# The down projection of a SwiGLU feed-forward layer as seven block products instead of eight, with its operands streamed from DRAM

## The chip, the cores and the metric

The kernel runs on one core of one Trainium2 chip. The time is device microseconds of one execution of the whole kernel, from a launch to its end. Before the change it took 2273.01 us, the median of three runs (2272.06 to 2274.47).

## The reference

The reference is one inference step of a two-layer decoder trunk over 1024 prompt tokens and 64 sample tokens (1088 rows), D_MODEL = 1024, all in float32. Layer 0 is a gMLP mixer, layer 1 a sliding-window attention; each has a SwiGLU feed-forward (D_FF = 2816) behind it, in sandwich RMSNorm:

```
def swiglu_ffn(h, w_gate, w_up, w_down):
    return (jax.nn.silu(h @ w_gate) * (h @ w_up)) @ w_down
...
        h = rms_norm(x, f_norm_pre[layer])
        x = x + rms_norm(swiglu_ffn(h, f_w_gate[layer], f_w_up[layer], f_w_down[layer]), f_norm_post[layer])
```

The change is about the last product, hidden (1088 x 2816) times `f_w_down` (2816 x 1024), which is done twice, once in each layer.

## The kernel before

**Number format.** Every large product is done in three matmuls. A float32 operand is split into a high part (ScalarE, L275 or L510, a copy into the rounded format) and a low part (VectorE, L276 or L511, the difference), and high*high, low*high and high*low are summed in one PSUM bank. A matmul here has a 128x128 stationary and a 128x512 moving operand.

**Gate and up.** `ffn` (L1080) walks 22 steps q: gate and up weights of a pair of feature tiles in turn. Each step already uses a seven-product scheme (`part` called from `p1`, `p2`, `p657`, `p4`, `p3`). The hidden values of a pair of feature tiles (two tiles of 128 features, 1024 prompt tokens) stand in two `rows` tiles, of which there are two, so that the next pair's first write (the `keep` copy at L1117) waits until this pair's stores have landed. `store` (L1092) writes each 128x512 block to a DRAM tensor `hid`, one for each feature tile, four blocks for a pair.

**Down.** Below the gate and up steps, `fetch` (L1211) loads whole feature tiles of the hidden rows back (L1218) and splits them; `W` (class `Weights`) loads, splits and hands out the tiles of `f_w_down`, up to six ahead (`W.cap`). The 22 feature tiles go in six groups (`GROUPS`). For each group, each of the eight token blocks (and the sample rows as a ninth) and each half of the output columns, `down` (L1223) sums the group's products in one bank, and the bank is added to an accumulator in SBUF (L1240; L1238 copies in the first group). So the prompt takes 22 x 8 x 2 x 3 = 1056 matmuls in a layer and the sample rows 22 x 2 x 2 = 88, all at L1235.

**What follows.** In the last group, each finished block goes through `Exit.second` (L1037): sum of squares on ScalarE (L1040), the root on GpSimd (L863), two passes on VectorE (L1042, L1043), and a store. In layer 0 a second norm follows (squares, root, scaled copy), and once three blocks are there `Exit.turn` (L1057) turns them with transposes on TensorE and splits them for the key, value and query products, which take the token ranges c = 0, 1, 2 in this order. In layer 1 the store of the last block ends the kernel.

**What sets the order.** `Flow` keeps a clock of TensorE work as the program is written, and `flow.later(ns, fn)` puts side work that many nanoseconds on. The tile framework then places each engine's instructions by its own timeline. All DMAs are issued from SyncE, in order, and a DMA that waits holds up those behind it. The big SBUF tiles come from one pool of 40 (`act_tile`); PSUM has five banks called `bank` and three called `aux`.

## Time and profile before

| what | value |
|---|---|
| profiled execution | 2275.59 us, span 2273.9 us |
| median of three runs | 2273.01 us |
| TensorE (PE) busy | 2202.6 us, 97% of the span, 11392 matmuls |
| weight loads (PEld) | 1864.3 us, 82%, beside the matmuls |
| VectorE (DVE) busy | 1283.2 us, 56% |
| ScalarE (ACT) busy | 810.4 us, 36% |
| DMA | 194.69 MB, mean 86 GB/s |
| down projection, layer 0 / layer 1 | 855.9 to 1126.7 us / 1999.8 to 2264.2 us |

The profile is one execution, taken by the hardware profiler. Instructions stand under the line of the kernel that issued them. Matmuls overlap: one takes 0.39 us from end to end, but a new one starts every 0.23 us, so busy time and not the mean is what a matmul costs. "Idle before, releaser" names what an engine waited for ahead of a group. The granted clock of TensorE is given as a share of full speed. A "chain of waits" follows the last instruction back through whatever released each step.

### The profile page before, as it was taken

The page shows a single profiled execution, that of the slowest core. Times are in us where ns is not written, and L with a number is a line of the kernel's source. Part 1 is how long each engine was busy: PE and PEld are TensorE (multiplying, and loading weights), DVE is VectorE, ACT ScalarE, POOL GpSimd, SP SyncE. Part 2 cuts the span into 40 slices and gives each one's busy share as a digit, 9 for nine tenths or more (in the row PEclk, how much of TensorE's full clock was granted, in tenths as well). Part 3 has the DMA queues.
Part 4 walks back from the last instruction along what each step waited for, and adds up shares of the span by engine and source line. Part 5 has one row for each costly group of instructions (what it writes and reads, how often), then busy time and mean ns, then how long its engine had stood idle before and what let it go on. Part 6 is the DMA issues. An engine that isn't in the chain of part 4 may idle for free.

```text
span 2273.9 us, 29115 instructions
## 1 busy us (share of the span) xinstructions
PE 2202.6 (97%) x11392; PEld 1864.3 (82%) x11392; DVE 1283.2 (56%) x2081; ACT 810.4 (36%) x1647; POOL 182.3 (8%) x222
## 2 busy tenths in 40 slices
PE   8999996999999999999999999969999999999998
PEld 7999875888888887888898877758888888878886
DVE  5465448655655653545757774477565565535446
ACT  5234424322322333211566762234232332342112
POOL 2322210000000000000213320110000000000000
PEclk9999998999999999999999998979999999999999
DMA  4211332122222234223441111221222221343224
GB/s 147 57 38 38 96 106 86 61 71 90 76 64 89 76 106 138 91 77 104 136 118 43 47 60 57 98 88 64 74 85 63 80 86 62 97 143 109 77 86 143
DMA packets 138975, 194.69 MB, mean 86 GB/s; under 512 B 22051, under 2 KB 101653, under 8 KB 138838
## 3 DMA queue, kind: packets, MB, share of 16 engines
q1 hardware_dynamic: 138838, 192.84, 26.8%
q8 instruction: 89, 1.46, 0.3%
q14 instruction: 48, 0.39, 0.1%
HBM read 143.88 MB, written 43.32 MB: 82 GB/s over the span
## 4 chain that ended last, share of the span: by engine, by line
PE 73%; DVE 5%; DMA 3%; ACT 2%; issue 1%; SPq 0%; POOL 0%; POOLq 0%; ACTq 0%; DVEq 0%
PE bank L1235 22%; PE bank L1076 11%; PE bank L1077 11%; PE bank L1078 11%; PE bank L1138 2%; PE bank L1137 2%; PE bank L873 2%; PE bank L874 1%; PE bank L505 1%; PE bank L504 1%; PE bank L506 1%; PE bank L875 1%; DVE act L276 1%; DMA act<-hid 1%; DMA raw<-in_f_w_down 1%
## 5 line engine op out<-in xcount | busy, mean ns | idle before, releaser
L1235 PE MATMUL bank<-act,act 128*128 128x512 f32 x2288 | 526.5, 392 | 5.9 <-ACT act L510 5.3
L1076 PE MATMUL bank<-act,act 128*128 128x512 f32 x1232 | 487.0, 396 | 31.0 <-ACT rows L1117 17.9
L276 DVE TENSOR_TENSOR act<-raw,act 128x1024 fp32r<-128x1024 f32 x261 | 317.5, 1223 | 352.0 <-PE bank L1077 188.3
L1235 PEld LDWEIGHTS bank<-act,act 128*128 128x128 f32 x2288 | 430.0, 189 | 100.7 <-ACT act L510 7.8
L275 ACT ACTIVATE act<-raw 128x1024 fp32r<-128x1024 f32 x261 | 275.2, 1059 | 597.7 <-PE bank L1235 203.9
L1077 PE MATMUL bank<-act,act 128*128 128x512 f32 x1232 | 485.2, 394 | 0.0
L1078 PE MATMUL bank<-act,act 128*128 128x512 f32 x1232 | 478.6, 391 | 1.2 <-DVE act L276 1.2
L1076 PEld LDWEIGHTS bank<-act,act 128*128 128x128 f32 x1232 | 232.8, 189 | 78.4 <-ACT rows L1117 18.3
L1078 PEld LDWEIGHTS bank<-act,act 128*128 128x128 f32 x1232 | 232.6, 189 | 51.0 <-DVE act L276 2.7
L1077 PEld LDWEIGHTS bank<-act,act 128*128 128x128 f32 x1232 | 233.2, 189 | 43.1
L1240 DVE TENSOR_TENSOR act<-bank,act 128x512 f32<-128x512 f32 x180 | 123.5, 688 | 150.9 <-PE bank L1235 150.7
L504 PE MATMUL bank<-act,act 128*128 128x384 f32 (+1 forms) x624 | 205.8, 332 | 2.0 <-DVE act L636 1.4
L506 PE MATMUL bank<-act,act 128*128 128x384 f32 (+1 forms) x624 | 206.8, 332 | 0.4 <-DVE act L276 0.4
L505 PE MATMUL bank<-act,act 128*128 128x384 f32 (+1 forms) x624 | 206.4, 331 | 0.0
L863 POOL TENSOR_TENSOR tok<-tok,expo 128x1 f32<-128x1 f32 (+1 forms) x63 | 54.5, 866 | 1719.3 <-DVE tok L862 1719.3
L504 PEld LDWEIGHTS bank<-act,act 128*128 128x128 f32 x624 | 117.7, 189 | 4.0 <-DVE act L636 1.6
L506 PEld LDWEIGHTS bank<-act,act 128*128 128x128 f32 x624 | 117.6, 189 | 1.9 <-issue 1.2
L505 PEld LDWEIGHTS bank<-act,act 128*128 128x128 f32 x624 | 117.8, 189 | 1.0 <-issue 0.7
L873 PE MATMUL bank<-act,act 128*128 128x512 f32 (+1 forms) x288 | 114.9, 402 | 0.6 <-DVE tok L899 0.6
L874 PE MATMUL bank<-act,act 128*128 128x512 f32 (+1 forms) x288 | 113.7, 395 | 0.0
L875 PE MATMUL bank<-act,act 128*128 128x512 f32 (+1 forms) x288 | 111.8, 393 | 0.0
L511 DVE TENSOR_TENSOR act<-act,act 128x64 fp32r<-128x64 f32 (+3 forms) x114 | 71.9, 657 | 49.9 <-ACT act L510 49.3
(231 smaller groups left out, 2628.0 us busy)
## 6 DMA issues: line engine op xcount, KB each, us to landing
act<-hid SPq DMA_DIRECT2D x44, 544.0 KB
raw<-in_f_w_gate SPq DMA_DIRECT2D x44, 512.0 KB
raw<-in_f_w_up SPq DMA_DIRECT2D x44, 512.0 KB
hid<-rows SPq DMA_DIRECT2D x88, 256.0 KB
raw<-in_f_w_down SPq DMA_DIRECT2D x44, 512.0 KB
stream<-act SPq DMA_DIRECT2D x24, 512.0 KB
rows<-stream SPq DMA_DIRECT2D x24, 512.0 KB
raw<-in_sg_w_in SPq DMA_DIRECT2D x16, 512.0 KB
```

Of the source, the lines that this page charges most:

```text
L275: nc.scalar.activation(self.hi, raw, AF.Copy)
L276: nc.vector.tensor_tensor(self.lo, raw, self.hi.bitcast(F32), op=ALU.subtract)
L504: nc.tensor.matmul(out[:, :n], h, xh[:, cs:cs + n], start=begin, stop=False)
L505: nc.tensor.matmul(out[:, :n], h, xl[:, cs:cs + n], start=False, stop=False)
L506: nc.tensor.matmul(out[:, :n], l, xh[:, cs:cs + n], start=False, stop=end)
L873: nc.tensor.matmul(ps[:m, :], xh, h, start=begins and j == 0, stop=False)
L874: nc.tensor.matmul(ps[:m, :], xl, h, start=False, stop=False)
L875: nc.tensor.matmul(ps[:m, :], xh, l, start=False, stop=ends and j == len(todo) - 1)
L1076: nc.tensor.matmul(ps, h, xh, start=begin and k == 0, stop=False, skip_group_check=not begin)
L1077: nc.tensor.matmul(ps, h, xl, start=False, stop=False, skip_group_check=not begin)
L1078: nc.tensor.matmul(ps, l, xh, start=False, stop=k == 3, skip_group_check=not begin)
L1235: nc.tensor.matmul(ps, x, w, start=i == j == 0, stop=i == n - 1 and j == len(todo) - 1)
```

## The change

With the feature tiles of a pair called 1 and 2, the first and second 512 tokens x and y, and the first and second 512 output columns u and v, the down projection becomes a 2 x 2 block product. It is now done in seven products by Strassen's scheme (in Winograd's form), each over 11 pairs and four token blocks: x1 u1, x2 u2, s3 t3, s2 t2, y2 t4, s1 t1, s4 v2, with s1 = y1+y2, s2 = s1-x1, s3 = x1-y1, s4 = x2-s2, and t1 = v1-u1, t3 = v2-v1, t2 = t3+u1, t4 = u2-t2.

- **Sums of the hidden blocks.** `sums` makes s1 to s4 of a pair after its last block (four 128x512 operations on VectorE); seven blocks of a pair are stored (x1, x2, y2, s1, s2, s3, s4) in place of four. The `rows` tiles of a pair are now taken at `p2`, and the `keep` copy of `p1` goes to a temporary.
- **Streaming.** Each product runs through six units of two pairs (the last of one). `send` loads a unit's hidden blocks and one or two quarter blocks of `f_w_down`; `make` splits the hidden blocks, forms t1 to t4 on VectorE, and splits the weights. Up to four units are sent ahead and two made ahead. `f_w_down` no longer goes through `W`, whose `cap` is 0 until the last product.
- **Sums in PSUM.** Four banks hold the four token blocks of a product through all 11 pairs; x2 u2 adds to the banks of x1 u1, and s1 t1 and s4 v2 add to those of s2 t2. `gather` joins products on ScalarE or VectorE, 28 times in a layer; the additions at L1240 are gone. The sample rows go with x1 u1, x2 u2, s1 t1 and s4 v2.
- **Exit.** `Exit` is split in `first` (the first half of the columns, after y2 t4) and `second`. Blocks 4 to 7 finish after s1 t1, blocks 0 to 3 after s4 v2, whose last four units are run block by block. In layer 0 the order of the last blocks is 3, 0, 1, 2, and the key, value and query products take the token ranges in the order 2, 1, 0.

The matmuls of a prompt layer come to 7 x 11 x 4 x 3 = 924 in place of 1056, those of the sample rows stay 88. The diff, cut to its core:

```
@@ -29,9 +29,11 @@
-GROUPS = [3, 3, 4, 4, 4, 4]
+SENT = 4
+STREAMED = 4
 ORDER = [0, 1, 2, 3, 8, 4, 5, 6, 7]
+CORDER = [2, 1, 0]
...
     def add_ffn(layer):
         for q in range(NF):
             W.add_quad(a[("f_w_gate", "f_w_up")[q % 2]][layer], q // 2 * 2, (layer, q))
-        for f in range(NF):
-            W.add(a["f_w_down"][layer][f * P:(f + 1) * P, :], 1, D)
...
+        def first(self, b, z):
+            m = tokens(b)
+            j = tmp()[:m, :]
+            nc.scalar.activation(j, z[:m, :HN], AF.Square, accum_out=tok[:m, 0, b:b + 1])
+            nc.vector.tensor_tensor(z[:m, :HN], z[:m, :HN], self.post[:m, :HN], op=ALU.mult)
+            nc.vector.tensor_scalar(tok[:m, 1, b:b + 1], tok[:m, 0, b:b + 1], 1.0 / D, EPS, op0=ALU.mult, op1=ALU.add)
...
         def second(self, b, z):
             m = tokens(b)
             h = act_tile()[:, :D]
             z, r = z[:m, :], self.r.pop(b)[:m, :]
-            nc.scalar.activation(h[:m, :], z, AF.Square, accum_out=tok[:m, 2, b:b + 1])
-            rs = inverse(b, 3, tok[:m, 2, b:b + 1], EPS)
-            nc.vector.scalar_tensor_tensor(z, z, rs, self.post[:m, :], op0=ALU.mult, op1=ALU.mult)
-            nc.vector.tensor_tensor(z, z, r, op=ALU.add)
+            nc.scalar.activation(h[:m, :HN], z[:, HN:], AF.Square, accum_out=tok[:m, 2, b:b + 1])
+            nc.vector.tensor_tensor(z[:, HN:], z[:, HN:], self.post[:m, HN:], op=ALU.mult)
+            rs = inverse(b, 3, tok[:m, 2, b:b + 1], tok[:m, 1, b:b + 1])
+            nc.vector.scalar_tensor_tensor(z, z, rs, r, op0=ALU.mult, op1=ALU.add)
...
-            if c == 0:
+            if k == len(self.x):
                 self.x.append(act_pair())
...
-        hid = [mk(dpool, [P, T], F32, f"hid{layer}_{f}") for f in range(NF)]
+        hid = {n: mk(dpool, [P, NF // 2, HN], F32, f"hid{layer}_{n}") for n in ("x1", "x2", "y2", "s1", "s2", "s3", "s4")}
+        hsm = mk(dpool, [P, 2, NF // 2, NS], F32, f"hid{layer}_smp")
...
         def store(q, i, c):
-            nc.sync.dma_start(hid[q // 2 * 2 + i][:, c * HN:(c + 1) * HN], region(q, i, c))
+            if i or not c:
+                nc.sync.dma_start(hid[("x" if c == 0 else "y") + str(i + 1)][:, q // 2, :], region(q, i, c))
+        def sums(q):
+            p = q // 2
+            x1, y1, x2, y2 = (region(q, i, c) for i in range(2) for c in range(2))
+            t = act_tile()
+            s1, s2 = t[:, :HN], t[:, HN:D]
+            for n, o, u, v, op in (("s1", s1, y1, y2, ALU.add), ("s3", y1, x1, y1, ALU.subtract),
+                                   ("s2", s2, s1, x1, ALU.subtract), ("s4", x1, x2, s2, ALU.subtract)):
+                nc.vector.tensor_tensor(o, u, v, op=op)
+                nc.sync.dma_start(hid[n][:, p, :], o)
...
         def p1(q):
             need("x1")
-            if q % 2 == 0:
-                rows[q // 2] = [special([P, D], "rows", bufs=2) for _ in range(2)]
+            if q == 0:
+                rows[0] = new_rows()
             s = st[q]
             s["a"] = bank()
             part(s["a"], unit(q, "b1"), 0, ent, "x1", True)
-            s["keep"] = region(q, 0, 1) if q % 2 == 0 else tmp()
+            s["keep"] = region(q, 0, 1) if q == 0 else tmp()
             nc.scalar.activation(s["keep"], s["a"], AF.Copy)
 
         def p2(q):
             need("x2")
             s = st[q]
             part(s["a"], unit(q, "b2"), 0, ent, "x2", False)
+            if q % 2 == 0 and q:
+                rows[q // 2] = new_rows()
             r = region(q, 0, 0)
             if q % 2 == 0:
                 nc.scalar.activation(r, s["a"], AF.Silu)
...
-                for i in range(2):
-                    nc.sync.dma_start(hid[q // 2 * 2 + i][:, SEQ:], r[:, i, :])
+                nc.sync.dma_start(hsm[:, :, q // 2, :], r)
...
             take(q, 0, 1, s["c"], s["u2"])
+            if q % 2:
+                sums(q)
...
+        wd = a["f_w_down"][layer].rearrange("(q i p) n -> p q i n", i=2, p=P)
+        order = [("x1", "u1"), ("x2", "u2"), ("s3", "t3"), ("s2", "t2"), ("y2", "t4"), ("s1", "t1"), ("s4", "v2")]
+        NP = NF // 2
+        units = [(hn, wn, e, min(2, NP - e)) for hn, wn in order for e in range(0, NP, 2)]
+        loaded, ready, chained, smps, ext = deque(), deque(), {}, {}, []
+        sent, made = [0], [0]
+        def send():
+            hn, wn, e, n = units[sent[0]]
+            sent[0] += 1
+            lo = act_tile(F32R)[:, :n * HN]
+            load(lo.bitcast(F32), hid[hn][:, e:e + n, :], n)
+            raws = []
+            for name in {"t3": ("v2", "v1"), "t2": ("u1",), "t4": ("u2",), "t1": ("v1", "u1")}.get(wn, (wn,)):
+                raws.append(act_tile()[:, :n * HN])
+                load(raws[-1], quarter(name, e, n), n)
+            loaded.append((lo, raws))
...
+        def make():
+            hn, wn, e, n = units[made[0]]
+            made[0] += 1
+            lo, raws = loaded.popleft()
+            hi = act_tile(F32R)[:, :n * HN]
+            split(hi, lo, lo.bitcast(F32))
+            c = raws[0]
+            if wn in ("t3", "t1"):
+                nc.vector.tensor_tensor(c, c, raws[1], op=ALU.subtract)
+            elif wn == "t2":
+                c = chained[e]
+                nc.vector.tensor_tensor(c, c, raws[0], op=ALU.add)
+            elif wn == "t4":
+                nc.vector.tensor_tensor(c, c, chained.pop(e), op=ALU.subtract)
+            if wn == "t3":
+                chained[e] = c
+            wh, wl = (t[:, :n * HN] for t in act_pair())
+            split(wh, wl, c)
+            ready.append((hi, lo, wh, wl))
...
+        def supply():
+            while sent[0] < min(len(units), made[0] + SENT):
+                send()
+            make()
...
+        def sample_rows(i):
+            smps[i] = []
...
+                nc.sync.dma_start(raw, hsm[:, i, e:e + n, :])
+                split(sm[:, :, 0, :], sm[:, :, 1, :], raw)
+                smps[i].append(sm.rearrange("p f s t -> p f (s t)"))
...
+            for e in range(n):
+                xh, xl = (t[:, e * HN + i * P:e * HN + (i + 1) * P] for t in (hi, lo))
+                h, l = (t[:, e * HN:(e + 1) * HN] for t in (wh, wl))
+                for k, (x, w) in enumerate([(xh, h), (xl, h), (xh, l)]):
+                    nc.tensor.matmul(ps, x, w, start=begin and e == k == 0, stop=end and e == n - 1 and k == 2,
+                                     skip_group_check=adds)
...
+            def gather(hn, i, ps):
+                (x0, x1), (y0, y1) = half[i], half[4 + i]
+                if hn in ("x1", "x2"):
+                    nc.scalar.activation(x1 if hn == "x1" else x0, ps, AF.Copy)
+                else:
+                    d, t = {"s3": (y1, x1), "s2": (y0, y1), "y2": (y0, y0), "s1": (y1, y1), "s4": (x1, x1)}[hn]
+                    nc.vector.tensor_tensor(d, ps, t, op=ALU.add)
...
+            rest = ([0, 1, 2, 3] if last else [3, 0, 1, 2])
...
+            for j, (hn, wn, e, n) in enumerate(units):
+                begin, end = e == 0, e + n == NP
+                if begin:
+                    if hn in ("x1", "s2"):
+                        A = [bank() for _ in range(4)]
+                    if hn in ("s3", "y2"):
+                        B = [bank()] + [aux() for _ in range(3)]
+                    if hn in ("x1", "s1"):
+                        sb = aux()
+                    if hn in ("x1", "x2"):
+                        sample_rows(int(hn[1]) - 1)
...
+                    if hn == "s4":
+                        W.cap = 2
+                        W.prepare()
+                u = ready.popleft()
+                if made[0] < len(units):
+                    supply()
...
+                if hn == "s4" and e >= STREAMED:
+                    kept.append((u, n, end))
+                    if not end:
+                        continue
+                    for i in rest:
+                        for u, n, end in kept:
+                            product(ps[i], i, u, n, False, end, True)
+                        gather(hn, i, ps[i])
+                        finish(i, acc[i])
+                        flow.run()
+                    continue
+                for i in range(4):
+                    product(ps[i], i, u, n, begin and not adds, end, adds)
+                    if end:
+                        gather(hn, i, ps[i])
+                        if hn == "y2":
+                            ext[0].first(4 + i, acc[4 + i])
+                            ext[0].first(i, acc[i])
+                        if hn == "s1":
+                            finish(4 + i, acc[4 + i])
+                    flow.run()
+            W.cap = 4
+            W.prepare()
...
+            if (fn, q) == (p2, NF - 1):
+                W.cap = 0
+                down_begin()
...
+        down()
+        return ext[0]
...
-    for c in range(3):
+    for c in CORDER:
...
-            if c == 2:
+            if c == CORDER[-1]:
```

Two places of the order are spoken of below. The first is SyncE at the start of the down projection of layer 0. `hid0_20` and `hid0_21` are the last two feature tiles, `rs` the sample rows' hidden values; the rows of before are:

```order
L1218 DMA act_1078_7005<-hid0_0_527_3407 128x1088
L349 DMA raw_1066_6992<-in_f_w_down 128x1024
L1093 DMA hid0_21_548_3428<-rows_1012_6630 128x512
L1218 DMA act_1080_7012<-hid0_1_528_3408 128x1088
L1093 DMA hid0_21_548_3428<-rows_1012_6630 128x512
L1163 DMA hid0_20_547_3427<-rs_1035_6802 128x64
L1163 DMA hid0_21_548_3428<-rs_1035_6802 128x64
L1093 DMA hid0_20_547_3427<-rows_1011_6629 128x512
L1218 DMA act_1082_7019<-hid0_2_529_3409 128x1088
```

The sample rows' part went to the same tensors as the rest, two DMAs for a pair. Now, at the same place, `hid0_smp` is a tensor of its own, stored for all pairs and read back at once (L1289):

```order
L1106 DMA hid0_x1_527_3407<-rows_1026_6771 128x512
L1243 DMA act_1059_6949<-hid0_x1_527_3407 128x1024
L1243 DMA act_1060_6951<-in_f_w_down 128x2x512
L1106 DMA hid0_y2_529_3409<-rows_1027_6772 128x512
L1106 DMA hid0_x2_528_3408<-rows_1027_6772 128x512
L1191 DMA hid0_smp_534_3414<-rs_1041_6868 256x1x64
L1289 DMA tmp_1090_7087<-hid0_smp_534_3414 128x512
L1289 DMA tmp_1092_7092<-hid0_smp_534_3414 128x192
L1289 DMA tmp_1124_7322<-hid0_smp_534_3414 128x512
L1289 DMA tmp_1126_7327<-hid0_smp_534_3414 128x192
L1117 DMA hid0_s1_530_3410<-act_1074_7063 128x512
L1243 DMA act_1093_7096<-hid0_x1_527_3407 128x512
```

The stores of the last pair are mixed with the loads of the first product, whose operand x1 was stored long before, and four reads of the sample rows follow their last store directly.

The second place is TensorE at the end of the down projection of layer 0. L1235 is the down projection of before, L1062 are transposes of `turn`, L504 and L505 the key products. Before:

```order
L1235 MATMUL bank_8760<-act_8370,act_8140 128x512
L1062 MATMUL aux_8664<-ident_70,act_8425 128x128
L1062 MATMUL aux_8664<-ident_70,act_8466 128x128
L1062 MATMUL aux_8664<-ident_70,act_8507 128x128
L1235 MATMUL bank_8833<-act_8078,act_8119 128x512
L1235 MATMUL bank_8833<-act_8078,act_8120 128x512
...
L1235 MATMUL bank_8847<-act_8369,act_8141 128x512
L1235 MATMUL bank_8847<-act_8370,act_8140 128x512
L504 MATMUL bank_8899<-act_8593,act_8375 128x384
L505 MATMUL bank_8899<-act_8594,act_8375 128x384
L506 MATMUL bank_8899<-act_8593,act_8376 128x384
```

The transposes stood among the matmuls of the down projection, and the last of these was followed by key products. After, where L1303 is the down projection and L1070 the transposes:

```order
L1303 MATMUL bank_7787<-act_8631,act_8543 128x512
L1303 MATMUL bank_7787<-act_8632,act_8628 128x512
L1070 MATMUL aux_8775<-ident_70,act_8670 128x128
L1070 MATMUL aux_8775<-ident_70,act_8474 128x128
L1070 MATMUL aux_8775<-ident_70,act_8491 128x128
...
L1070 MATMUL aux_8807<-ident_70,act_8525 128x128
L1070 MATMUL aux_8807<-ident_70,act_8694 128x64
L1070 MATMUL aux_8813<-ident_70,act_8670 128x128
L1070 MATMUL aux_8813<-ident_70,act_8474 128x128
L1070 MATMUL aux_8813<-ident_70,act_8491 128x128
L504 MATMUL bank_8940<-act_8779,act_6903 128x320
L504 MATMUL bank_8975<-act_8779,act_8536 128x320
```

Eighteen transposes now stand between the last matmul of the down projection and the first key product, and the rest of the turning goes on among the key products.

More of the change, by code (lines that the diff above doesn't have):

```diff
@@ L1104, in take, with new_rows @@
                 store(q, i, c)
+        def new_rows():
+            return [special([P, D], "rows", bufs=2) for _ in range(2)]
         def need(name):
@@ new lines, in down_begin, with product @@
+        def down_begin():
+            for i in range(2):
+                supply()
+        def product(ps, i, u, n, begin, end, adds):
+            hi, lo, wh, wl = u
+            for e in range(n):
[4 more added lines that the diff above has]
+                                     skip_group_check=adds)
+            flow.pe(n * 3 * HN / 2.4)
@@ L1242, in folded @@
-        def folded():
-            for h in range(2):
-                ps = bank()
-                nc.tensor.matmul(ps[:NS, :], fold, acc[NB][:, h * HN:(h + 1) * HN], start=True, stop=True)
-                nc.scalar.activation(z8[:NS, h * HN:(h + 1) * HN], ps[:NS, :], AF.Copy)
-            flow.pe(1800)
-            ext.second(NB, z8)
-        fetch(0)
-        for gi, gn in enumerate(GROUPS):
-            xs, hs = parts.popleft()
-            us = [W.get() for _ in range(gn)]
-            order = list(range(NB + 1))
-            final = gi == len(GROUPS) - 1
-            if final:
-                W.cap = 5
-                ext = Exit(lambda b: ent.out[:tokens(b), b, :], ("f_norm_post", layer), last)
-                order = [NB] + order[:-1] if last else order[:6] + [NB] + order[6:-1]
-                ext.fetch(order[0])
-                z8 = act_tile()[:, :D]
-            for j, b in enumerate(order):
-                if final and j < NB:
-                    ext.fetch(order[j + 1])
-                for h in range(2):
-                    down(b, h, us, xs, hs, gi)
-                    if j == NB and h:
-                        for u in us:
-                            W.done(u)
-                    flow.run()
-                if j == 0 and not final:
-                    fetch(gi + 1)
-                if final and b < NB:
-                    ext.second(b, acc[b])
-                elif final:
-                    flow.later(K["zsum"], folded)
@@ L1277, in ffn @@
-        return ext
+        down()
+        return ext[0]
     def widen():
```

89 lines of the change are left out of this document (57 added, 32 removed).

## The prediction

> **What bounds the kernel now.** I read the page first: the busy times, the chain that ended last, and the largest group.
>
> ```profile
> PE 2202.6 (97%) x11392; PEld 1864.3 (82%) x11392; DVE 1283.2 (56%) x2081; ACT 810.4 (36%) x1647; POOL 182.3 (8%) x222
> PE 73%; DVE 5%; DMA 3%; ACT 2%; issue 1%; SPq 0%; POOL 0%; POOLq 0%; ACTq 0%; DVEq 0%
> L1235 PE MATMUL bank<-act,act 128*128 128x512 f32 x2288 | 526.5, 392 | 5.9 <-ACT act L510 5.3
> ```
>
> TensorE is busy for 97% of the span and carries the chain. The group that the change rewrites, L1235, holds 526.5 us, and TensorE idled only 5.9 us ahead of it. Then the windows by stage (gate and up, down, and what follows, in layer 0; gate and up, down in layer 1) say whether other engines have room there.
>
> ```profile
> core 0: us, PE busy (x) PEld busy (x) DVE busy (x) ACT busy (x) POOL busy (x), PEclk, DMA share, GB/s
> 410.00:856.00 446.00, 443.43 (x2127) 371.85 (x2125) 258.57 (x348) 140.50 (x205) 0.00 (x0) 1.00 0.26 81
> 856.00:1127.00 271.00, 268.02 (x1173) 219.42 (x1174) 132.50 (x187) 75.28 (x116) 7.78 (x11) 0.99 0.31 106
> 877.00:1127.00 250.00, 250.00 (x1111) 205.81 (x1110) 122.86 (x172) 66.41 (x99) 7.78 (x11) 1.00 0.28 96
> 1127.00:1200.00 73.00, 73.00 (x463) 70.56 (x462) 45.98 (x90) 50.72 (x114) 14.98 (x16) 1.00 0.45 121
> 1552.00:1995.00 443.00, 441.65 (x2121) 370.63 (x2120) 257.20 (x345) 139.98 (x204) 0.00 (x0) 1.00 0.25 78
> 2025.00:2264.00 239.00, 239.00 (x1051) 196.54 (x1050) 118.58 (x161) 50.62 (x74) 4.40 (x8) 1.00 0.30 101
> ```
>
> Behind its first 20 us the down projection runs with TensorE busy for 250.00 of 250.00 us and 239.00 of 239.00, at full granted clock. VectorE has half of that time free, ScalarE more, the DMA engines some 70%. So a matmul less is time less, as long as the new work of the others stays under the rate of the matmuls.
>
> **Matmuls.** A layer loses 1056 - 924 = 132, both 264. One costs 526.5/2288 = 0.230 us of busy time; the window 2025:2264 gives 239.00/1051 = 0.227. That is -59.9 to -60.7; I take **-60.0**. All of it lies on the path.
>
> **Start of the down projection.** The timeline of TensorE there, start and length in us, and two windows:
>
> ```profile
> 855.93 7.71 PE L1235 MATMUL bank<-act,act 128*128 128x512 f32 x30 [1.18 <-ACT act L510]
> 866.56 13.77 PE L1235 MATMUL bank<-act,act 128*128 128x512 f32 x47 [2.92 <-ACT act L510]
> 2008.94 1.43 PE L1235 MATMUL bank<-act,act 128*128 128x512 f32 x5 [1.22 <-ACT act L510]
> 864.00:873.00 9.00, 6.44 (x16) 5.09 (x17) 2.15 (x4) 4.00 (x8) 0.00 (x0) 0.62 0.63 243
> 867.00:870.00 3.00, 3.00 (x8) 2.32 (x8) 0.76 (x1) 0.05 (x1) 0.00 (x0) 0.50 0.86 352
> ```
>
> TensorE waits 1.18 + 2.92 + 1.22 = 5.3 us for reloaded, split hidden rows, and behind the 2.92 us gap the granted clock stands at 0.50: in 864:873 sixteen matmuls took 6.44 us, where 16 x 0.230 = 3.7 would do, 2.7 more. The Trainium skill (TensorE: Matmul & The Clock Gate, Part 1: The HAM clock gate) has the clock halve after at least one idle window of about 3.4 us; by that a gap of 2.92 us costs no clock, and this term would be -5.3. The row shows 0.50 behind the shorter gap, so the row decides. The first product's operand x1 was stored long before and is loaded ahead, so these waits should go: **-8.0**. What is late next: the last pair's stores and the four reads of the sample rows, one queue on SyncE, in which a read waits for the store in front of it; the sample rows' split waits for that, and so do the sample matmuls that stand in x1 u1, with the first units behind. From nothing up to one round trip more than before, 0 to 6 for each layer (bounded by the two gaps plus the loss, 1.18 + 2.92 + 2.7 = 6.8). Other matmuls of x1 u1 can stand ahead of them, so I take 1 each: **+2**.
>
> **Steady flow of units.** A unit of two pairs is 2 x 4 x 3 = 24 matmuls, 5.5 us. Its work on VectorE goes by these rows:
>
> ```profile
> L276 DVE TENSOR_TENSOR act<-raw,act 128x1024 fp32r<-128x1024 f32 x261 | 317.5, 1223 | 352.0 <-PE bank L1077 188.3
> L1240 DVE TENSOR_TENSOR act<-bank,act 128x512 f32<-128x512 f32 x180 | 123.5, 688 | 150.9 <-PE bank L1235 150.7
> L275 ACT ACTIVATE act<-raw 128x1024 fp32r<-128x1024 f32 x261 | 275.2, 1059 | 597.7 <-PE bank L1235 203.9
> ```
>
> Two low parts and, for t1 to t4, one sum, all 128x1024, make 3 x 1.22 = 3.7 us; a product's four gathers, 4 x 0.69 over six units, add 0.5: 4.1 of 5.5. ScalarE has two copies, 2.1. VectorE goes from half to three quarters in the middle products and is not the bound. The 180 additions of L1240 go, 28 gathers a layer come, at the same 0.69. A bank is handed on when its gather is done; four banks end one behind another, 6 matmuls (1.4 us) apart, twice the gather's time. So hidden, at most one eviction of 0.7 for each change of banks, some ten of them: 0 to 7, I take **+1**.
>
> **Transfers.** Per layer 7 x 11 hidden blocks and 9 x 11 quarter blocks of 0.262 MB are loaded, 20.2 + 25.9 = 46.1 MB. Before:
>
> ```profile
> act<-hid SPq DMA_DIRECT2D x44, 544.0 KB
> raw<-in_f_w_down SPq DMA_DIRECT2D x44, 512.0 KB
> 853.50:856.00 2.50, 1.32 (x8) 0.75 (x6) 1.03 (x4) 1.32 (x3) 0.00 (x0) 1.00 0.96 261
> 860.00:864.00 4.00, 3.64 (x15) 2.48 (x15) 1.02 (x1) 0.00 (x0) 0.00 (x0) 1.00 1.00 334
> ```
>
> That was 22 x (0.557 + 0.524) = 23.8 MB, and 271 us at 106 GB/s are 28.7, so 4.9 MB of others. After: 51 MB in some 240 us, 212 GB/s. Busy engines moved 334 GB/s at a share of 1.00 and 261 at 0.96, and the gate and up stage's 81 GB/s at 0.26 come to 311 at full share. The tightest products are s3 t3 and s1 t1 with three transfers of 0.524 MB a unit: 1.57/5.5 = 286 GB/s (s1 t1 less, 44 sample matmuls stand in it). At 261 the 8.65 MB of s3 t3 take 33.1 us against 30.4 of matmuls: 3 per layer late. Four units are sent ahead during x2 u2, which needs 191 GB/s. So 0 to 6 for both layers, I take **0**.
>
> **Gate and up.** The sums add 44 VectorE operations a layer and three stores a pair, and `rows` are taken at `p2`, so the Silu there waits for the former pair's last store, s4, behind it the rest of ScalarE's queue.
>
> ```profile
> L1103 DVE TENSOR_TENSOR rows<-tmp,rows 128x512 f32<-128x512 f32 x66 | 45.3, 686 | 0.8
> L1117 ACT ACTIVATE rows<-bank 128x512 f32<-128x512 f32 x22 | 13.1, 597 | 29.4 <-DMA hid<-rows 25.5 <-DVE rows L1103 3.8
> ```
>
> 44 x 0.69 = 30 us beside VectorE's 258.57 of 446.00: it fits. ScalarE already waited 25.5 us for such stores in 22 turns, while TensorE was busy 443.43 of 446.00 and 441.65 of 443.00, so such a wait is mostly covered by matmuls on other banks. If the cover goes it is a store's wait, 25.5/22 = 1.2, in a third of 22 pairs: 8. Range 0 to 8, I take **+1**.
>
> **End of layer 0.** Before, key products follow the last matmul at once:
>
> ```profile
> 1123.14 3.90 PE L1235 MATMUL bank<-act,act 128*128 128x512 f32 x16
> 1126.89 0.33 PE L504 MATMUL bank<-act,act 128*128 128x384 f32 x1
> L510 ACT ACTIVATE act<-aux 128x512 fp32r<-128x512 f32 (+4 forms) x121 | 58.8, 514 | 75.4 <-PE aux L949 24.8 <-PE aux L570 17.8 <-PE aux L1579 15.5
> L1040 ACT ACTIVATE act<-act 128x1024 f32<-128x1024 f32 (+1 forms) x18 | 19.0, 1058 | 42.9 <-DVE act L1240 42.9
> ```
>
> Now 18 transposes stand first, and the turning of the other blocks among the key products. ScalarE's work over that stretch is some 16 copies of L510 (16 x 0.514 = 8.2) and six of 128x1024 (scaled copies, squares, weight copies; 6 x 1.06 = 6.4), 14.6 us, begun about 3 us late behind gather and root. TensorE has about 114 instructions beside it, by 73.00/463 = 0.158 us each 18 us. So 17.6 against 18: between no stall, and 10, if the first key product waits for two thirds of ScalarE's work (two thirds of 14.6). I take **+4**.
>
> **End of the kernel.** The last block of before:
>
> ```profile
> 2264.95 0.68 DVE L1240 TENSOR_TENSOR act<-bank,act 128x512 f32<-128x512 f32 x1
> 2265.66 1.06 ACT L1040 ACTIVATE act<-act 128x1024 f32<-128x1024 f32 x1 [4.29 <-DVE act L1240]
> 2267.73 1.28 DVE L1042 SCALAR_TENSOR_TENSOR act<-act,tok,act 128x1024 f32<-128x1024 f32 x1 [0.73 <-POOL tok L863]
> 2269.05 1.23 DVE L1043 TENSOR_TENSOR act<-act,rows 128x1024 f32<-128x1024 f32 x1
> ```
>
> The squares fall to half the width, 1.06 to about 0.6 (L1117's copy of 128x512), and one of the two passes of VectorE goes, 1.23: **-1.7**. The multiplication by the norm's weights lies beside the squares.
>
> **The sum.** -60.0 - 8.0 + 2 + 1 + 0 + 1 + 4 - 1.7 = -61.7. From the profiled execution's 2275.6 that is 2213.9; the median of the runs shown lies 2.6 lower, so 2211.3, said as **2212**. With every open term at its best end (-60.7 - 8.0 - 1.7 = -70.4) it is 2202.6.
>
> **Rivals.** *Transfers do not overlap enough; slower than before.* Chance 0.05. In the chain of waits ahead of the down projection of layer 0:
>
> ```profile
> 839.82 4.21 DMA raw<-in_f_w_down
> 846.46 3.55 DMA raw<-in_f_w_down
> ```
>
> A 0.524 MB transfer took 3.55 to 4.21 us, 148 to 125 GB/s. If transfers of that size, one behind another in SyncE's one queue, keep about 148, the 51 MB take 345 us where 271 stood: +74 a layer, 2273 + 148 = 2421. It decides below 51/271 = 188 GB/s. Against it speak the rows of 334 and 352 GB/s with the same kinds of transfers in flight together, and up to four units sent ahead. The Trainium skill (DMA: Bandwidth & Descriptors, Anatomy of one DMA) gives a transfer issued by GpSimd about 2.0 us fixed plus its bytes at 436 GB/s; if that were paid in series, 3.2 us for 0.524 MB and 164 GB/s, the estimate would be 311 us a layer, 2353. The two lone transfers lie near that price, the windows of 334 and 352 say that it is not paid in series.
>
> *The ends wait.* The turn takes its 10 and halves the clock once (+2.7 as in 864:873), and both starts take their 6: 8.7 + 10 over the sum, 2230. For it: 18 transposes ahead of the key products, and the sample rows' round trip; against it: ScalarE's and TensorE's work are about even there. Chance 0.15.
>
> *The change does not do what it says*: fewer matmuls, but each unit waits for its split operands. To give back 62 us over 2 x 42 units each must wait 0.74, so VectorE's 4.1 us of a unit must become 6.2, half as much again. Nothing in 877:1127, where VectorE's operations run at their mean beside full matmuls, shows such a stretch. No change; chance 0.03.
>
> **How the numbers follow.** The forecast has 0.77. About 0.2% is what a measurement of this kernel can tell from no change. The forecast and the waiting ends are both faster by far: 0.92; 0.03 for the same, 0.05 slower. The range reaches from the best end, 2202, past the waiting ends at 2230 with the gate and up term's 8 (7 more than taken) and 3 of transfers: 2240; it leaves out the other two rivals and the sum of all mishaps.
>
> **What would show it.** In the profile after: 264 fewer matmuls at 0.227 to 0.230 us, 2024 at the line of the down projection; windows inside both down projections with TensorE busy throughout at clock 1.00, VectorE near 60 to 75%, DMA share 0.6 to 0.7; no wait over 1 us at their start, or one on the sample rows' read; a gap of some 4 us ahead of the first key product of layer 0; the gate and up windows as long as before. A DMA share near 1 with gaps ahead of s3 t3 and s1 t1, or a clock under 1 between products, would say that the transfers or the hand-overs cost more; gate and up longer by over 5 us that the stores do.

## The result, and the profile after

The changed kernel takes 2205.97 us, the median of four runs (2203.36 to 2208.61), against 2272.53 us for the kernel before in the same series: a ratio of 0.9706, 95% interval 0.9689 to 0.9723, 66.6 us less. The forecast was 2212 in a range of 2202 to 2240. The profiled execution took 2203.92 us with a span of 2202.2, against 2275.59 and 2273.9 before. Spans differ by 71.7 us, 5 more than medians: one profiled execution lies 3 above its median, the other 2 below. The terms below are compared in the profiles.

The page of the kernel after, busy times, chain and the groups of the new down projection:

```profile
PE 2136.6 (97%) x11128; PEld 1815.8 (82%) x11128; DVE 1381.0 (63%) x2159; ACT 867.8 (39%) x1711; POOL 192.7 (9%) x222
PE 37%; DVE 2%; issue 1%; ACT 0%; POOL 0%; POOLq 0%; ACTq 0%
L1303 PE MATMUL bank<-act,act 128*128 128x512 f32 x1452 | 342.2, 389 | 0.0
```

11392 - 11128 = 264 instructions of TensorE are gone, VectorE is up from 56% to 63% of a shorter span, and TensorE idled 0.0 us ahead of the down projection, 5.9 before. (Its matmuls into the other PSUM tiles and for the sample rows, 396 and 176, are groups of their own.)

Windows of the kernel after: gate and up of layer 0; down, what follows and the next stretch; gate and up, down and the end of layer 1. The columns are those of the windows of before.

```profile
347.50:846.70 499.20, 480.75 (x2328) 402.42 (x2327) 334.15 (x461) 165.96 (x249) 4.27 (x6) 0.98 0.30 98
846.70:1084.20 237.50, 237.50 (x1043) 194.81 (x1042) 156.39 (x187) 107.11 (x148) 17.34 (x12) 1.00 0.65 218
1084.20:1310.20 226.00, 221.91 (x1661) 204.40 (x1660) 153.50 (x385) 149.12 (x493) 47.88 (x54) 0.97 0.25 67
1457.00:1955.10 498.10, 479.66 (x2316) 401.76 (x2315) 327.93 (x455) 164.06 (x247) 4.65 (x6) 0.98 0.30 97
1955.10:2192.60 237.50, 237.50 (x1044) 194.68 (x1042) 154.73 (x182) 93.73 (x132) 12.90 (x8) 1.00 0.63 214
2192.60:2202.20 9.60, 0.24 (x2) 0.00 (x0) 3.99 (x5) 0.72 (x2) 0.55 (x1) 0.70 0.49 200
```

Both down projections are busy from the first matmul to the last, 237.50 of 237.50 us at full clock, with the DMA engines at 0.63 to 0.65 and VectorE at 156.39/237.50 = 66%. The last row, from the last matmul on, is as long as before.

The gain, stage by stage. Windows of before from the first gate and up matmul to the last down matmul, in layer 0 and in layer 1, and from there to the end:

```profile
348.10:1126.90 778.80, 754.71 (x3526) 626.17 (x3525) 440.78 (x612) 243.12 (x368) 11.96 (x17) 0.98 0.27 88
1493.90:2264.40 770.50, 748.01 (x3489) 619.97 (x3488) 435.33 (x598) 229.20 (x347) 9.06 (x14) 0.98 0.28 89
2264.40:2273.90 9.50, 0.17 (x1) 0.00 (x0) 3.90 (x5) 1.15 (x2) 0.55 (x1) 0.72 0.27 110
```

The first two of these stretches in the kernel after:

```profile
347.50:1084.20 736.70, 718.25 (x3369) 597.23 (x3368) 490.54 (x648) 273.06 (x397) 21.62 (x18) 0.99 0.41 137
1457.00:2192.70 735.70, 717.26 (x3357) 596.44 (x3356) 482.66 (x636) 257.78 (x379) 17.56 (x14) 0.99 0.41 135
```

That is -42.1 us and -34.8 us for gate, up and down. Part of it comes back between the two stretches, before and after:

```profile
1126.90:1493.90 367.00, 361.18 (x2398) 306.08 (x2396) 228.21 (x542) 199.38 (x638) 74.53 (x76) 0.97 0.26 75
1084.20:1457.00 372.80, 363.01 (x2423) 310.33 (x2421) 227.95 (x546) 198.62 (x641) 67.72 (x74) 0.96 0.25 74
```

This is 5.8 us more. The transposes that stood inside the down projection of layer 0 (24 of them within its last 25 us) now stand behind it; their own work is some 2 us of that, by the 0.24 us that three of them took between matmuls before. The rest is a gap ahead of the key products, in which they wait.

**The start.** TensorE's timeline of after, at the first down matmuls of layer 0:

```profile
846.65 5.38 PE L1303 MATMUL bank<-act,act 128*128 128x512 f32 x23
851.87 0.39 PE L1084 MATMUL bank<-act,act 128*128 128x512 f32 x1
```

Windows of 30 us at the starts of both down projections, before:

```profile
846.80:876.80 30.00, 24.45 (x94) 18.46 (x93) 15.50 (x23) 11.59 (x22) 0.00 (x0) 0.89 0.66 228
1993.70:2023.70 30.00, 28.26 (x118) 21.42 (x119) 13.79 (x21) 13.57 (x25) 0.00 (x0) 1.00 0.59 202
```

and after:

```profile
844.70:874.70 30.00, 30.00 (x135) 24.81 (x134) 18.41 (x25) 10.13 (x13) 0.00 (x0) 1.00 0.74 261
1955.10:1985.10 30.00, 30.00 (x136) 24.79 (x135) 20.16 (x26) 12.43 (x16) 0.00 (x0) 1.00 0.66 237
```

The first unit's matmuls (L1303) now run ahead of the last 24 gate and up matmuls (L1084 to L1086), in the very place where TensorE had waited 1.39 us for L1181 (1.35 in layer 1). In 30 us, 94 and 118 matmuls started before, 135 and 136 now: 41 x 0.227 = 9.3 us and 18 x 0.227 = 4.1 us won, more than the waits that the timeline named.

**The gap.** TensorE behind the last matmul of layer 0, after:

```profile
1077.95 6.43 PE L1303 MATMUL bank<-act,act 128*128 128x512 f32 x27
1084.21 1.15 PE L1070 MATMUL aux<-ident,act 128*128 128x128 f32 x9
1086.82 1.10 PE L1070 MATMUL aux<-ident,act 128*128 128x128 f32 x6 [1.46 <-DVE act L511]
1090.49 0.90 PE L1070 MATMUL aux<-ident,act 128*128 128x128 f32 x3 [2.57 <-DVE act L511]
1091.04 0.88 PE L504 MATMUL bank<-act,act 128*128 128x320 f32 x2
```

and a window of after just behind:

```profile
1090.50:1093.90 3.40, 3.40 (x13) 2.87 (x14) 1.91 (x5) 1.58 (x4) 0.55 (x1) 0.51 0.38 157
```

The gap is 7.0 us from the start of the last down matmul to the first key product, 4.03 of them idle, and behind it the granted clock stands at half for one stretch of some 3.4 us (0.51 in the window). Below, "the gap" is counted in this way in each version, and "the end" from the start of the last matmul to the end of the span (9.7 us before and after); both are read to about 0.1 us.

### The profile page after: what moved, and what is told of

Same layout as the page of the kernel before. It is cut to its first block, busy times and chain, and to the rows that moved or that the text cites. A ratio compares the mean times of both kernels' runs of the same rounds, so it can differ in the third digit from the quotient of the medians.

```text
span 2202.2 us, 29096 instructions
## 1 busy us (share of the span) xinstructions
PE 2136.6 (97%) x11128; PEld 1815.8 (82%) x11128; DVE 1381.0 (63%) x2159; ACT 867.8 (39%) x1711; POOL 192.7 (9%) x222
## 5 line engine op out<-in xcount | busy, mean ns | idle before, releaser
L1084 PE MATMUL bank<-act,act 128*128 128x512 f32 x1232 | 487.2, 397 | 28.3 <-ACT rows L1144 18.0
L1085 PE MATMUL bank<-act,act 128*128 128x512 f32 x1232 | 485.4, 394 | 0.0
L1086 PE MATMUL bank<-act,act 128*128 128x512 f32 x1232 | 475.8, 392 | 1.2 <-DVE act L278 1.2
L278 DVE TENSOR_TENSOR act<-raw,act 128x1024 fp32r<-128x1024 f32 x217 | 265.3, 1227 | 239.1 <-ACT act L277 73.3
L277 ACT ACTIVATE act<-raw 128x1024 fp32r<-128x1024 f32 x217 | 226.7, 1058 | 307.4 <-DVE raw L298 190.7
L1303 PE MATMUL bank<-act,act 128*128 128x512 f32 x1452 | 342.2, 389 | 0.0
L1303 PEld LDWEIGHTS bank<-act,act 128*128 128x128 f32 x1452 | 272.2, 188 | 59.6 <-issue 1.6
L1084 PEld LDWEIGHTS bank<-act,act 128*128 128x128 f32 x1232 | 233.1, 189 | 75.1 <-ACT rows L1144 18.3
L1086 PEld LDWEIGHTS bank<-act,act 128*128 128x128 f32 x1232 | 232.9, 189 | 51.2 <-DVE act L278 2.7
L1085 PEld LDWEIGHTS bank<-act,act 128*128 128x128 f32 x1232 | 233.5, 189 | 43.1
L510 ACT ACTIVATE act<-act 128x1024 fp32r<-128x1024 f32 (+5 forms) x194 | 166.7, 905 | 182.6 <-PE bank L1303 62.0
L511 DVE TENSOR_TENSOR act<-act,act 128x1024 fp32r<-128x1024 f32 (+5 forms) x194 | 194.1, 1039 | 50.5 <-ACT act L510 44.5
L504 PE MATMUL bank<-act,act 128*128 128x384 f32 (+1 forms) x624 | 206.9, 334 | 2.1 <-DVE act L636 1.4
L863 POOL TENSOR_TENSOR tok<-tok,expo 128x1 f32<-128x1 f32 (+1 forms) x63 | 65.8, 1051 | 1624.8 <-DVE tok L862 1624.8
L505 PE MATMUL bank<-act,act 128*128 128x384 f32 (+1 forms) x624 | 206.6, 332 | 0.0
L504 PEld LDWEIGHTS bank<-act,act 128*128 128x128 f32 x624 | 117.7, 189 | 4.4 <-DVE act L636 1.6
L505 PEld LDWEIGHTS bank<-act,act 128*128 128x128 f32 x624 | 118.1, 189 | 1.1 <-issue 0.9
L506 PEld LDWEIGHTS bank<-act,act 128*128 128x128 f32 x624 | 117.8, 189 | 1.0 <-DVE act L278 0.7
```

What stands on the lines that cost most here:

```text
L277: nc.scalar.activation(self.hi, raw, AF.Copy)
L278: nc.vector.tensor_tensor(self.lo, raw, self.hi.bitcast(F32), op=ALU.subtract)
L504: nc.tensor.matmul(out[:, :n], h, xh[:, cs:cs + n], start=begin, stop=False)
L505: nc.tensor.matmul(out[:, :n], h, xl[:, cs:cs + n], start=False, stop=False)
L506: nc.tensor.matmul(out[:, :n], l, xh[:, cs:cs + n], start=False, stop=end)
L510: nc.scalar.activation(hi, src, AF.Copy)
```

## The experiments

The theory to be tested: the saved matmuls carry 60 us, the waits at the start 13 more, the turn gives some back, and neither the transfers nor VectorE come near the bound inside the products. The rivals: the streaming and not the count carries the gain; the transfers or VectorE are at their limit. The kernel before was measured again beside each group of experiments, with medians from 2274.48 to 2275.16 us where it had 2272.53 beside the change. So versions that lie a few microseconds apart are told apart by their profiles, stage by stage, and not by their medians.

### Eight products, streamed

```
-            if q % 2:
-                sums(q)
...
-        order = [("x1", "u1"), ("x2", "u2"), ("s3", "t3"), ("s2", "t2"), ("y2", "t4"), ("s1", "t1"), ("s4", "v2")]
+        order = [("x1", "u1"), ("x2", "u2"), ("y1", "u1"), ("y2", "u2"), ("y1", "v1"), ("y2", "v2"), ("x1", "v1"), ("x2", "v2")]
...
```

> The streaming, the split exit and the order of the end are kept, the seven products are undone: eight products x1 u1, x2 u2, y1 u1, y2 u2, y1 v1, y2 v2, x1 v1, x2 v2, no sums of hidden blocks, no t1 to t4, four stores a pair, 264 matmuls more; the loads are the same 176 blocks a layer. Theory (the saved matmuls carry the gain at 0.227 us each, the sums hide): 2206 + 60 = 2266, some 6 under the kernel before, whose waits at the start of the down projection stay away. Rival (the streaming itself carries a good part, by a better fed TensorE or shorter hand-overs): 2220 to 2250. Rival (the seven products' sums cost hidden time): above 2266 is impossible by it, 2255 to 2263 if they cost 3 to 11.

Measured: 2260.17 us (2258.36 to 2261.74), ratio to before 0.9936 (0.9918 to 0.9954). Its windows, cut as above:

```profile
347.90:1116.00 768.10, 748.73 (x3510) 622.61 (x3509) 445.60 (x588) 286.66 (x416) 18.40 (x21) 0.99 0.37 122
1486.20:2252.00 765.80, 746.24 (x3489) 620.42 (x3488) 435.64 (x569) 269.46 (x390) 16.02 (x14) 0.98 0.36 120
2251.80:2259.90 8.10, 0.38 (x2) 0.00 (x0) 2.79 (x4) 0.72 (x2) 0.55 (x1) 0.67 0.33 136
```

In layer 1, with the same other work on TensorE, the stretch is 765.80 - 735.70 = 30.1 us longer than after, for 132 matmuls: 0.228 each, the price that was taken. Against before it is 770.50 - 765.80 = 4.7 shorter with the same 3489 instructions: that is for the most part the start (4.1 by counting). The median lies 54 over the changed kernel and not 60, as the third theory had it, but not for its reason: the products cost their full 30 us a layer, and the difference lies at the ends, 2.7 us ahead of the key products in place of 7.0 (9 transposes of the turn still stand inside the down projection) and 8.1 in place of 9.7 at the end. (The spans of the two profiled executions lie 57.7 apart: 31.4 and 30.1 us in the two stretches, less 2.6 between them and 1.6 at the end. What is left to 54 is the spread of the runs.) Streaming, with the exit and the order that come with it, is worth 15 us by itself, against the kernel before in the same series; the seven products are worth the rest, some 52.

### The transfers' margin

```
+            if hn in ("x2", "s2", "y2", "s4"):
+                load(act_tile()[:, :n * HN], quarter("v1", e, n), n)
```

> x2 u2, s2 t2, y2 t4 and s4 v2 load a second quarter block of the weights in each unit that nothing reads: 44 blocks of 0.262 MB, 11.5 MB a layer more, so that nearly every unit loads three times 0.524 MB, 286 GB/s at the pace of the matmuls. Theory (transfers have room: busy engines move 330 to 400 GB/s): plus 0 to 3. Rival (some 261 GB/s is what they sustain, so the change runs just under the bound): the stretch of 210 us grows by a tenth, plus 20 a layer, 2246.

Measured: 2206.78 us (2204.75 to 2211.41). A window inside each down projection:

```profile
880.00:1050.00 170.00, 170.00 (x751) 140.77 (x751) 108.30 (x119) 70.52 (x93) 0.00 (x0) 1.00 0.85 291
1990.00:2085.00 95.00, 95.00 (x421) 78.69 (x420) 55.88 (x55) 38.19 (x46) 0.00 (x0) 1.00 0.86 307
```

291 and 307 GB/s at shares of 0.85 and 0.86, and TensorE without a gap; both stretches of gate, up and down are as long as after to 0.1 us. So 261 GB/s was no ceiling, and the 218 of the change leave room.

### How far ahead

```
-SENT = 4
+SENT = 2
```

> At most two units are sent ahead, as many as are made, in place of four. Theory (transfers of a unit overlap and take some 5 us, one unit of matmuls 5.5, so with two in flight or made the loads still come in time in most products; s3 t3 with three transfers a unit, t2 and t4 less, wait): plus 5 to 40. Rival (lookahead is not needed at all): plus 0 to 2. Rival (each unit waits a whole transfer of 3.6 to 4.2 us with its split): plus 100 or more.

Measured: 2209.44 us (2208.13 to 2214.58). The theory was wrong: inside the products nothing waits (both stretches of gate, up and down are as long as after to 0.1 us). What is longer is the gap of layer 0, 11.0 us for 7.0, and the end, 10.6 for 9.7. At the end VectorE's work stands in another order: the last pass of the block in front comes behind the last addition from PSUM and waits 1.85 us for its residual rows. Why sending fewer units ahead leads to that order is not shown.

### Without the early first units

```
-                down_begin()
             flow.run()
+        down_begin()
         down()
```

> The first two units are sent and made behind the last gate and up step and not ahead of its last four parts. Theory (the early first units are what takes away the waits at the start, which cost the kernel before some 9 us in layer 0 and 4 in layer 1): a load of 4 us and a split of 2.3 come back in front of each down projection, partly beside the scheduler's other work, and the clock may halve: plus 8 to 20. Rival (the waits of before came from the last pair's stores and the reload behind them, and x1, stored long ago, is there at once in any order): plus 0 to 3.

Measured: 2231.87 us (2231.20 to 2237.16), 26 more, above the 8 to 20 that were expected. TensorE's timeline at the first down matmul of each layer:

```profile
868.20 1.22 PE L1303 MATMUL bank<-act,act 128*128 128x512 f32 x2 [10.41 <-ACT act L510]
1992.31 2.93 PE L1303 MATMUL bank<-act,act 128*128 128x512 f32 x6 [10.99 <-ACT act L510]
```

and its windows, cut as above:

```profile
352.20:1102.20 750.00, 720.11 (x3369) 597.96 (x3369) 491.20 (x649) 274.09 (x397) 21.64 (x18) 0.98 0.40 134
1476.80:2225.80 749.00, 718.36 (x3357) 596.62 (x3356) 483.36 (x636) 258.75 (x379) 17.57 (x14) 0.98 0.40 133
```

13.3 us more in each layer, of which 10.41 and 10.99 are the wait for the splits of the first unit. In layer 0 the split that ends last is that of the weights, behind their load, and the clock is at half behind it:

```profile
867.09 1.06 ACT L510 ACTIVATE act<-act 128x1024 fp32r<-128x1024 f32 x1 [1.07 <-DMA act<-in_f_w_down]
868.20:872.50 4.30, 4.30 (x10) 3.44 (x11) 2.42 (x2) 1.95 (x2) 0.00 (x0) 0.50 1.04 410
```

The high part of x1 was ready 2.1 us earlier. The half clock, 4.3 us here and 3.2 in layer 1, makes up most of the rest. It is not enough that x1 was stored long ago: the load and split of the first unit, of its weights too, have to be written ahead of the last gate and up parts.

### VectorE's margin

The low part of the weights once more in each unit, and in a second kernel twice more:

```
             split(wh, wl, c)
+            nc.vector.tensor_tensor(wl, c, wh.bitcast(F32), op=ALU.subtract)
```

> The low part of the weights is computed twice in each unit, one VectorE operation of 128x1024, 1.22 us, more. A unit of s3 to s1 then has 3 x 1.22 + 0.5 + 1.22 = 5.4 us of VectorE in the 5.4 us of its 24 matmuls. Theory (VectorE has a quarter of the time free and two units of lead): plus 0 to 8. Rival (VectorE is already close to setting the pace, its waits for ScalarE's copies eat the rest): plus 1.22 in most of 84 units, 40 to 90.

> The low part of the weights is computed three times, 2.44 us of VectorE more in each unit: 6.6 us in a unit of s3 to s1, 5.4 in the others (no sum of weights). Theory: VectorE sets the pace in s3 t3, s2 t2, y2 t4 and s1 t1, 24 units a layer by about 1.2 (s1 t1, with the sample rows' matmuls, by less), less two units of lead: plus 20 to 26 a layer, 2246 to 2258. Rival (something else hides it): under 20 in all.

Measured: 2215.10 us (2214.26 to 2216.93) and 2262.29 (2261.77 to 2271.14). A window inside the down projection of layer 0, with one more:

```profile
960.00:1060.00 100.00, 100.00 (x440) 81.89 (x439) 87.95 (x107) 46.90 (x67) 8.83 (x5) 1.00 0.64 211
```

and with two more:

```profile
960.00:1060.00 100.00, 88.86 (x365) 70.83 (x364) 95.98 (x108) 35.66 (x49) 0.00 (x0) 0.95 0.58 187
```

With VectorE at 88% TensorE still has no gap; the 9 us come from the ends alone, a gap of 12.8 for 7.0 and an end of 13.9 for 9.7. With two more, VectorE is at 96% and TensorE at 89% in the window, and gate, up and down take 28.5 and 26.6 us more. That is near the 20 to 26 expected, but not where the theory had it. Windows over s3 t3 and s1 t1 of layer 0 in that kernel:

```profile
932.80:962.70 29.90, 29.90 (x133) 24.77 (x132) 29.34 (x28) 11.40 (x14) 0.00 (x0) 1.00 0.47 158
1029.90:1075.40 45.50, 39.48 (x157) 30.81 (x156) 40.44 (x52) 17.28 (x31) 0.00 (x0) 0.92 0.43 135
```

In s3 t3 VectorE is busy for 98% and TensorE still loses nothing, as the theory's two units of lead would have it; s1 t1 takes 45.5 us, where its 154 matmuls ask for 35.0. By counting starts in all products, s3 t3 to s1 t1 lose 17 us in layer 0 and 15 in layer 1, and x1 u1 with s4 v2 lose another 11 in each, which the theory had at nothing. So the total came near partly by luck. VectorE is the next bound: inside the products, one 128x1024 operation a unit more fits and two do not.

### Which range first

```
-CORDER = [2, 1, 0]
+CORDER = [1, 2, 0]
```

> Key, value and query products of layer 1 take the token ranges in the order 1, 2, 0 in place of 2, 1, 0. Range 1 (blocks 3, 4, 5) is scaled at 1081.2 us in the profile after, range 2 waits for the sample rows, scaled at 1087.6. Theory (the stall of 1.46 + 2.57 us and a half-clock stretch of 3.4 us behind the down projection of layer 0 come from the sample rows' late end): the stall shrinks to 0 to 2 us, 2201 to 2204. Rival (the stall is the ScalarE work of turning as a whole, whatever range comes first): 2205 to 2207.

Measured: 2202.22 us (2200.00 to 2205.05), ratio 0.9685 (0.9666 to 0.9703). TensorE behind the last down matmul of layer 0:

```profile
1084.86 1.15 PE L1070 MATMUL aux<-ident,act 128*128 128x128 f32 x9
1086.88 0.62 PE L504 MATMUL bank<-act,act 128*128 128x384 f32 x2 [0.87 <-ACT act L510]
1087.47 0.55 PE L1070 MATMUL aux<-ident,act 128*128 128x128 f32 x3
```

The gap is 2.3 us for 7.0, and no stretch at half clock follows it. The runs overlap with those of the changed kernel, and so do the intervals of the ratios; the shorter gap, 4.7 us, is of the size of the medians' 3.8. No version that was run has a lower median.

### Early residual rows, and the sample rows first

The residual rows into tiles of the big pool, up to four ahead; alone, and with the new order of ranges:

```
-        fetch = Enter.fetch
+        def fetch(self, b):
+            self.r[b] = act_tile()[:, :D]
+            nc.sync.dma_start(self.r[b][:tokens(b), :], self.res(b))
...
-                if ahead and len(e.r) < 2:
+                while ahead and len(e.r) < 4:
```

> The residual rows of the blocks' last pass are loaded into tiles of the big pool, up to four ahead, in place of two rows tiles that each wait for an earlier block's last pass. Theory (the end of the kernel gained nothing because a VectorE pass waited 2.49 us for such a load in front of the last eviction, and 1.46 us of the stall behind layer 0 have the same cause): the end, 9.7 us from the last matmul on, falls to about 8.1 as with eight products, the gap ahead of the first key product from 7.0 to 5.5: 2203. Rival (the loads come late because the transfers of s4 v2 stand in front of them, whatever tile they go to): no change, 2206.

> The order 1, 2, 0 of the token ranges and the early residual rows together. Theory (two separate waits): the gains add, 2200 to 2201. Rival (the residual wait in layer 0 is the same stall that the order took away): the end's 1.6 alone adds, 2200.5 to 2202; if the early loads gain nothing by themselves, 2202.

Measured: 2207.12 us (2206.06 to 2208.06) and 2203.38 (2201.84 to 2203.71): nothing gained. The wait for the load that the theory named is there in the kernel after, and gone in the one with early rows. VectorE at the end, after:

```profile
2193.12 1.29 DVE L1051 SCALAR_TENSOR_TENSOR act<-act,tok,rows 128x1024 f32<-128x1024 f32 x1 [2.49 <-DMA rows<-stream]
2194.32 0.68 DVE L1325 TENSOR_TENSOR act<-bank,act 128x512 f32<-128x512 f32 x1
```

and with early rows alone:

```profile
2195.25 1.28 DVE L1053 SCALAR_TENSOR_TENSOR act<-act,tok,act 128x1024 f32<-128x1024 f32 x1 [0.66 <-POOL tok L863]
2196.45 0.68 DVE L1327 TENSOR_TENSOR act<-bank,act 128x512 f32<-128x512 f32 x1
```

The last eviction (L1325, L1327, the addition that takes a finished bank out of PSUM) still stands behind the last pass of the block in front of it, which now waits for the root: the end is 9.0 and 9.2 us, not 8.1. Alone, the early rows also change the order behind layer 0 (24 transposes stand ahead of the first key product, not 18), and the gap grows to 12.1. The theory on the end holds for the wait and falls for its worth.

With both, the sample rows' last passes were then written ahead of the first block's end:

```
                             product(ps[i], i, u, n, False, end, True)
+                        flow.run()
                         gather(hn, i, ps[i])
```

> The order 1, 2, 0, the early residual rows, and the sample rows' last passes written ahead of the first block's end and not behind it. Theory (what still keeps the end at 9.2 us in place of 8.1 is VectorE's passes over the sample rows and one block in front of the last evictions): end 8.1 to 8.5 us, gap ahead of the first key product 1 to 3: about 2201. Rival (the end is set by the last block's own passes alone): 9.2 us stays, 2202 to 2203.

Measured: 2213.86 us (2209.80 to 2214.49), 10 worse than without it. The end is 8.7, but TensorE behind layer 0 shows:

```profile
1085.65 0.39 PE L1072 MATMUL aux<-ident,act 128*128 128x128 f32 x2
1094.10 0.36 PE L1072 MATMUL aux<-ident,act 64*128 64x64 f32 x1 [8.06 <-ACT act L1061]
1096.18 1.63 PE L1072 MATMUL aux<-ident,act 128*128 128x128 f32 x6 [1.71 <-ACT act L1061]
```

The sample rows' first transpose (64x64) now stands third in TensorE's order and waits 8.06 us for the sample rows' scaled copy, and all the others stand behind it. This shows, from the other side, what the order of ranges had shown: the gap is set by which range is turned and used first, and the sample rows are late.

### Ends bunched

```
-STREAMED = 4
+STREAMED = 10
```

> Only the last unit of s4 v2, one pair, is run block by block; the units before it go unit by unit, so the four blocks end within 12 matmuls, 2.7 us, and not within 63, 14.3 us. Theory (a block's end takes 2.9 us of VectorE, an eviction and two passes, 0.69 + 0.69 + 1.28 and the root; what the block by block order hides comes back): end of the kernel 9.7 to 17 us, gap in layer 0 7 to 14 to 18, and a half clock: plus 14 to 22. Rival (the ends are ScalarE's and GpSimd's latency, not throughput, so bunching hurts little): plus 0 to 6.

Measured: 2229.19 us (2227.50 to 2233.54), 23 more, a little over the 14 to 22 expected: the gap of layer 0 is 21.2 us, the end 21.8, and both stretches of gate, up and down 1.2 to 1.3 shorter. The block by block end is worth that much.

## Why the prediction was right, point by point

- **Matmuls, -60.** Right in mechanism and size: 264 fewer, 30.1 us for 132 of them between two kernels that differ in little else.
- **Start, -8 + 2.** Right in mechanism, too small: -13 by counting starts, and up to -15 by the stretches (-42.1 - 34.8, less the 60 of the matmuls and the 2 of the transposes that moved out). The sum took the idle that the timeline names (5.3) and the clock's 2.7. Matmul records of 0.39 us every 0.227 overlap, so a short gap between starts is counted as busy; counting matmuls in 30 us against a full stretch gives 9.3 and 4.1. The wait for L1181 was not in the sum, and it went too, since the first unit moved into it. The +2 for the sample rows' round trip did not come: their matmuls (L1311) first start at 863.2, 16 us behind the first unit, and wait for nothing.
- **Steady flow, VectorE 4.1 of 5.5.** Right: no gap in either down projection, and one more operation per unit still hides. The +1 for hand-overs of banks was not needed: counting starts shows no loss at them either.
- **Transfers, 0.** Right, with more room than its range allowed.
- **Gate and up, +1.** The wait came, but elsewhere. The waits of after:

```profile
ACT rows L1154 <- DVE rows L1116: 148.6, 20, 9.2
```

  The Silu of `p2` waits for the last sum (L1116) to have read the tiles, 148.6 us in 20 turns, where 25.5 us had been waited for stores. TensorE does not see it: it is busy 480.75 us in the stretch of 499.20, and for the same work before it was busy 480.77 us, in a stretch that the wait for L1181 made longer:

```profile
348.10:848.80 500.70, 480.77 (x2328) 402.19 (x2326) 304.29 (x420) 165.28 (x248) 4.28 (x6) 0.98 0.25 77
```

- **End of layer 0, +4.** The size came out: the idle time is 4.03 us, and the 5.8 us between the stretches are about 4 without the work of the moved transposes. The reason did not, so the size was luck: that ScalarE's amount of work sets the gap was wrong, for with the same work in another order of ranges it falls to 2.3. A stretch at half clock follows, which the term did not have.
- **End of the kernel, -1.7.** Wrong: 0. The squares are shorter, 0.63 us for 1.06, and one pass is gone. But the multiplication by the norm's weights (L1049) does not lie beside the squares, as the prediction had it: it starts when they have ended.

```profile
2195.04 0.63 ACT L1048 ACTIVATE act<-act 128x512 f32<-128x512 f32 x1 [5.26 <-DVE act L1325]
2195.79 0.69 DVE L1049 TENSOR_TENSOR act<-act,act 128x512 f32<-128x512 f32 x1 [0.79 <-ACT act L1048]
```

  So from the last eviction to the last pass it is 2.95 us, where it was 2.78 to the first of two passes, and only the pass that went is saved: 7.9 us from the eviction to the end for 8.9. And the last eviction starts 1.9 us behind the start of the last matmul, where it was 0.8: it stands behind another block's pass, held by its residual rows. With eight products, where it starts 0.4 behind, the end is 8.1. That is 1.5 less than before, 1.2 from the eviction on and 0.3 from the earlier eviction, so it is not the sum that had been meant either.

Where the sum went: in the profiled executions 71.7 us were saved where 61.7 were forecast, 10 more; in the medians the forecast of 2212 was 6 too high. The start gave 7 to 9 more than its -6, gate and up and the hand-overs 1 each; against that the end gave 1.8 less. What is then open, some 1 to 3 us, is no more than the runs differ by (2203.36 to 2208.61). Of the rivals, the transfers fell with the runs at 291 to 307 GB/s, and the waiting units with a TensorE that has no gap; the waiting ends are there, at 4 us of idle time and not at 10.

The Trainium skill (TensorE: Matmul & The Clock Gate, Part 1: The HAM clock gate) asks for about 3.4 us idle before the clock halves. Here it fell behind idle stretches of 1.46 and 2.57 us with 1.1 us of transposes between, so again shorter gaps were enough. The Trainium skill (DMA: Bandwidth & Descriptors, Anatomy of one DMA) gives a fixed 2.0 us to each transfer that GpSimd issues. SyncE's transfers here did not pay such a time in series: 291 to 307 GB/s went through, for the most part in transfers of 0.524 MB.

## What to carry to other kernels

Where TensorE is busy without a gap, a matmul saved is worth its pitch, and the operands' sums are free inside the stage while every other engine keeps up with TensorE; here one more VectorE operation of 128x1024 a unit was still free there, and two more were not. Look for what is left at the seams: write the first loads and splits of a stage ahead of the last work of the one in front, and let what is ready first be used first behind it. Measure a stage's loss by counting starts against a full stretch, not by the idle that is printed.

## What was not expected of the hardware

- The DMA engines moved 291 to 307 GB/s over 95 to 170 us beside full matmuls, with 218 GB/s and 307 GB/s giving the same TensorE pace.
- Halving the units sent ahead changed nothing inside the products, though a lone transfer had taken 3.55 to 4.21 us.
